# A hybrid decoder layer: turning states and cached keys in 32x32 blocks on VectorE instead of with TensorE transposes

## The chip, the cores and the metric

The kernel runs on one core of one Trainium2 chip. The metric is the time of one execution in device microseconds; several executions are run and the median is given. A profile of one execution gives the span from its first to its last instruction, which is a little shorter than the execution's time.

## The reference

One inference step of one decoder layer, all in float32, for two groups of tokens at once: a prompt of 512 tokens and 8 samples of 4 tokens each, so 544 columns of 1024 features.

```python
proj = rmsnorm(x) @ w_in                      # x_r | q | k | v | two gates
xc, conv_state = causal_dwconv(x_r, lru_conv_prev, conv_w, conv_b)     # width 4
lru_out, h_last = rg_lru(xc, lru_h0, ...)     # 8 block-diagonal gate groups, a scan over time
attn = band_attention(q, [k_cache, k], [v_cache, v], ...)   # window 128, sinks, relative bias
m = (sigmoid(g_A) * (lru_out @ w_lru_o) + sigmoid(g_B) * (attn @ w_attn_o)) @ w_out
x = x + rmsnorm(m)
u, ffn_state = causal_dwconv(rmsnorm(x) @ w_up, ffn_prev, ffn_conv_w, ffn_conv_b)   # width 3
x = x + rmsnorm((gelu(u_gate) * u_val) @ w_down)
```

Beside the new x, the step returns its states, with the time or sample index as rows and the features contiguous: the last LRU state and the last three pre-convolution rows (`s_lru_h`, `s_lru_conv`, 8 and 24 rows of 1024 for the samples; `p_lru_h`, `p_lru_conv`, 1 and 3 rows for the prompt), the key and value windows, and the last two rows of the feed-forward convolution (`s_ffn_conv`, 16 rows of 8192 for the samples; `p_ffn_conv`, 2 rows). The same states of the step before are inputs, in the same layout (`state_lru_h`, `state_lru_conv`, `cache_win_k`, `state_ffn_conv`).

## The kernel before

Inside the kernel, features lie on the 128 partitions and tokens along the free dimension. The states come and go with features contiguous, so each must be turned. Before the change TensorE does this, multiplying by an identity matrix (`pe.transpose`), and VectorE or ScalarE copies the result out of PSUM:

- `params` (L599): 8 transposes of the LRU states (`ps_st`, L604), copied by VectorE into `stT` (L610).
- `sample_attn` (L867), once for each half `g` of the samples: 8 transposes of cached keys (`pkc`, L881), copied by ScalarE into `kcT` (L886), which the score products `pss` read.
- `lru_states` (L1025): two times 4 transposes of the new LRU states (`plr`, L1030), copied by VectorE into the raw buffer `lru_rows` (L1032), which four transfers issued by GpSimd (L1033 to L1036) write out.
- `ffn_prev` (L1508): 8 transposes of the old convolution rows (`psf`, L1513), copied by ScalarE into `sfT` (L1514).
- `ffn_states` (L1734): two times 8 transposes, of the new convolution rows of the samples (`pfs`, L1741) and of the prompt (`pfp`, L1742), copied by ScalarE (L1744, L1746) and written out by transfers that GpSimd issues (L1747, L1748).

Every large product is done in three float32r products (high by high, high by low, low by high): weights are loaded by SyncE into one of five raw buffers (`RAW`, 4 KB a partition), ScalarE writes the rounded high part (L283, L1462), VectorE the rest (L290, and `sub`, L168).

**Order of work.** The order on TensorE is written out by hand throughout, that of ScalarE, VectorE and GpSimd in the mixer too (until `mixer.close()`, L1147), and that of ScalarE and VectorE again in the feed-forward part. SyncE everywhere, GpSimd after the mixer, and ScalarE and VectorE between the two parts are put in order by the scheduler, which goes by the order of emission and its own estimates. The main loop emits one product step after another (`step`, L344; `slot`, L1589). After each, `tick` lets side generators run whose time has come: `start_at(t, gen)` starts one, and `yield k` puts its next piece k steps later. A step in the mixer is 24 matmuls; in the feed-forward part a slot of 12 matmuls counts half a step. Projections empty one of three PSUM buffers (`psm`, used by `PM`), other products and transposes use five (`psx`, `PX`). Slots of the pool `S` (53) hold most activations.

Feed-forward tiles come in pairs `p_` = 0 to 31, a value tile j = `p_` and a gate tile j = 32 + `p_`. `states(j)` (L1543) takes the old rows of tile j out of `sfT`, with m = j // 8 and c = j % 8, and puts the new rows in the same place. From `p_` = 6 on, a pair takes seven half-size products ("a11" to "a22") whose weight sums VectorE and accumulating transfers on GpSimd's queue form (`sums`, L1443; transfers L1450 and L1451). The last pair's convolution, gating and split follow the last products closely; then come eight last column tiles (`down`, with weights `dl`) and the final norms.

Of the kernel before, what the change touches and what calls it, by code (L numbers as in the profile page):

```python
# [11 lines left out]
F32 = mybir.dt.float32  # L12
# [111 lines left out]
def hawk_step(ctx, tc, I, O):  # L124
# [466 lines left out]

    st_rows = [S(f"st_rows{z}") for z in range(2)]
    for z, t_ in enumerate(st_rows):
        zs = slice(512 * z, 512 * z + 512)
        nc.sync.dma_start(out=t_[0:24, 0:512], in_=I["state_lru_conv"][0, :, :, zs].rearrange("b i d -> (b i) d"))
        nc.sync.dma_start(out=t_[24:32, 0:512], in_=I["state_lru_h"][0, :, zs])
    stT = cp.tile([P, KD, 32], F32, name="stT")

    def params():  # L599
        ps = PX("ps_rows")  # L600
        pe.transpose(ps[:, 0:96], rows_a[:, :], ident[:96, :96])
        px = PX("ps_st")
        for k in range(KD):
            pe.transpose(px[:, k * 32:(k + 1) * 32], st_rows[k // 4][:32, (k % 4) * P:(k % 4 + 1) * P], ident[:32, :32])  # L604
        for z in range(2):
# [3 lines left out]
        dve.tensor_copy(fv, ps[:, 128:384])  # L609
        dve.tensor_copy(stT, px[:, 0:256].rearrange("p (k r) -> p k r", k=KD))  # L610
        yield 2
# [255 lines left out]
    def sample_attn(g):  # L867
        raws, kcT = [], []
        for nme in ("cache_win_k", "cache_win_v"):
            t_ = RAW(f"{nme}{g}").rearrange("p (b x) -> p b x", b=4)  # L870
            nc.sync.dma_start(out=t_, in_=I[nme][0, 4 * g:4 * g + 4].rearrange("b j k d -> j b (k d)"))
            raws.append(t_)
        kraw, vraw = raws
        yield 2
        pxs = []
        for half in range(2):
            px = PX(f"pkc{g}{half}")
            for b in range(2):
                for kv in range(NKV):
                    c0 = (2 * b + kv) * P  # L880
                    pe.transpose(px[:, c0:c0 + P], kraw[:, 2 * half + b, kv * HD:(kv + 1) * HD], ident)  # L881
            pxs.append(px)
# [50 lines left out]

    stage = cp.tile([P, KD, 36], F32, name="stage")
    L = Full("l", HALF2)
# [68 lines left out]
    def lru_scan(c):  # L1004
# [17 lines left out]
        pool.tensor_copy(stage[:, c, 27:28], hs[:, SEQ - 1:SEQ])  # L1022
        pool.tensor_copy(stage[:, c, 28:36], hv[:, :, 3])

    def lru_states():  # L1025
        o_t = rp.tile([36, D], F32, tag="raw", name="lru_rows")
        for hf in range(2):
            px = PX(f"plr{hf}")
            for j in range(4):
                pe.transpose(px[:36, j * P:(j + 1) * P], stage[:, 4 * hf + j, :], ident)  # L1030
            yield
            dve.tensor_copy(o_t[:, hf * 512:(hf + 1) * 512], px[:36, :])  # L1032
        pool.dma_start(out=O["p_lru_conv"][0, 0], in_=o_t[0:3, :])  # L1033
        pool.dma_start(out=O["s_lru_conv"][0].rearrange("b i d -> (b i) d"), in_=o_t[3:27, :])
        pool.dma_start(out=O["p_lru_h"][0], in_=o_t[27:28, :])
        pool.dma_start(out=O["s_lru_h"][0], in_=o_t[28:36, :])  # L1036
        yield

# [314 lines left out]


    QL = 32 // CH - 1
    XOF = {"a11": "b11", "a12": "b21", "p2": "t2", "p3": "t3", "p1": "t1", "p4": "b22", "a22": "t4"}
# [145 lines left out]

    sfT = fp.tile([P, KD, 16, 8], F32, name="sfT")
    stage_p = fp.tile([P, KD, 2, 8], F32, name="stage_p")
# [3 lines left out]
    def ffn_prev():  # L1508
        for kk in range(2):
            px = PX(f"psf{kk}")  # L1510
            for j in range(4):
                k = 4 * kk + j
                pe.transpose(px[:, j * P:(j + 1) * P], sf_rows[:, k * P:(k + 1) * P], ident)  # L1513
            act.copy(sfT[:, 4 * kk:4 * kk + 4].rearrange("p c r m -> p c (r m)"),  # L1514
                     px.rearrange("p (c x) -> p c x", c=4))

# [26 lines left out]
    def states(j):  # L1543

        m, c = j // 8, j % 8
        uv = samples(ut[j])
        sv = sfT[:, c, :, m].rearrange("p (b i) -> p b i", b=DB)
# [185 lines left out]

    def ffn_states():  # L1734
        os_ = O["s_ffn_conv"].rearrange("o b i (m n) -> (o b i m) n", n=D)
        op = O["p_ffn_conv"].rearrange("o b i (m n) -> (o b i m) n", n=D)
        for kk in range(2):
            px = PX(f"pfs{kk}")
            py = PX(f"pfp{kk}")
            for j in range(4):  # L1740
                pe.transpose(px[:, j * P:(j + 1) * P], sfT[:, 4 * kk + j].rearrange("p r m -> p (r m)"), ident)  # L1741
                pe.transpose(py[:16, j * P:(j + 1) * P], stage_p[:, 4 * kk + j].rearrange("p r m -> p (r m)"), ident)  # L1742
            o1, o2 = S(f"ffn_rows_s{kk}"), S(f"ffn_rows_p{kk}")
            act.copy(o1[:, 0:512], px)  # L1744
            yield 0.5
            act.copy(o2[:16, 0:512], py[:16, :])  # L1746
            pool.dma_start(out=os_[:, kk * 512:(kk + 1) * 512], in_=o1[:, 0:512])  # L1747
            pool.dma_start(out=op[:, kk * 512:(kk + 1) * 512], in_=o2[:16, 0:512])  # L1748
            yield

# [3 lines left out]
    for z in range(0, len(early), 2):  # L1754
        for u in range(2):
            for j in early[z:z + 2]:
                plain("e", j, u, 0)
                slot(1, 0, nearly, True)
        if z == 6:
            ffn_prev()  # L1760
    at[0], s_ = nearly - AHEAD, 0
# [5 lines left out]
    for i, x in enumerate(plan):  # L1767
# [11 lines left out]
        if i == len(plan) - 8:  # L1779
            start_at(now[0] + 1, x1_again())  # L1780
            start_at(now[0] + 3, ffn_states())

# [197 lines left out]
```

## Time and profile before

| what | value |
|---|---|
| median of 3 runs | 991.0 us (990.68, 991.0, 991.62) |
| span of the profiled execution | 989.3 us |
| runs above the span of the profiled one | 1.4 to 2.3 us (its own time is not given apart) |
| moved by transfers | 135.62 MB, mean 137 GB/s |
| clock granted to TensorE | 0.998 of full speed |

In the views, `PE` is TensorE, `DVE` VectorE, `ACT` ScalarE, `POOL` GpSimd and `SP` SyncE. A row of the chain gives a start, a duration, an engine and a tile. A row of the timeline adds the operation, its shapes and, in brackets, the idle time of the engine just before and what ended it. A row of the groups gives busy time, mean nanoseconds of one, then idle time before. A row of the waits gives total, count and longest. `L168` is line 168, often that of a helper, so tiles tell more than lines.

### The profile page before, as it was taken

What the parts mean: (1) busy time and instruction counts of PE and PEld (TensorE: products, weight loads), DVE (VectorE), ACT (ScalarE), POOL (GpSimd) and SP (SyncE); (2) the same over time, 40 slices, a digit from 0 to 9 for tenths busy, and PEclk for the clock granted to TensorE, in tenths of its full rate; (3) what the DMA queues carried; (4) which work ended last, traced back from release to release, by engine and by line L of the source; (5) the groups of instructions that cost most, each with busy time, mean ns of one, the idle gap of its engine ahead of it and who ended that gap; (6) DMA issues with size and microseconds to landing.
All of it is one profiled execution on the core that took longest, in us unless ns stands there. A gap on an engine that the chain in (4) does not pass through costs nothing.

```text
span 989.3 us, 20126 instructions
## 1 busy us (share of the span) xinstructions
PE 979.6 (99%) x7780; PEld 971.6 (98%) x7780; DVE 746.8 (75%) x1610; ACT 558.3 (56%) x1356; POOL 160.9 (16%) x271
## 2 busy tenths in 40 slices
PE   9999999999999999999999999999999999999997
PEld 8999999999999999999999999999999999999996
DVE  6777678766848555689786778787888888879866
ACT  6545334468476435556766665555655555556652
POOL 2143000002506341210011010101010101011004
PEclk9999999999999999999999999999999999999999
DMA  7675222323223535236058586867676767668612
GB/s 213 187 231 174 81 70 86 107 86 106 87 66 107 176 113 151 60 129 192 13 126 178 136 180 140 177 143 175 145 169 152 168 152 166 155 154 198 197 47 91
DMA packets 211111, 135.62 MB, mean 137 GB/s; under 512 B 8965, under 2 KB 197133, under 8 KB 210984
## 3 DMA queue, kind: packets, MB, share of 16 engines
q1 hardware_dynamic: 198984, 112.59, 40.0%
q0 software_dynamic: 11920, 19.59, 11.9%
q10 hardware_dynamic: 112, 2.17, 0.6%
q8 instruction: 61, 1.00, 0.4%
q14 instruction: 34, 0.28, 0.1%
HBM read 111.78 MB, written 11.37 MB: 124 GB/s over the span
## 4 chain that ended last, share of the span: by engine, by line
PE 96%; DVE 2%; ACT 1%; issue 0%; DVEq 0%; POOL 0%; ACTq 0%; POOLq 0%
PE pmin L165 22%; PE pmdn L165 17%; PE pux L1525 16%; PE puy L1525 8%; PE pq L1525 6%; PE pmout L165 5%; PE pmao L165 5%; PE pmlo L165 5%; PE puz L1525 4%; PE pg L165 1%; PE psc L165 1%; PE pvp L165 1%; PE ptok L165 1%; PE pt L819 1%; PE ps_warm L165 0%
## 5 line engine op out<-in xcount | busy, mean ns | idle before, releaser
L165 PE MATMUL pmin<-hH,wh_in 128*128 128x256 f32 (+1 forms) x568 | 164.6, 292 | 0.0
L165 PE MATMUL pmin<-hL,wh_in 128*128 128x256 f32 (+1 forms) x568 | 162.3, 288 | 0.0
L165 PE MATMUL pmin<-hH,wl_in 128*128 128x256 f32 (+1 forms) x568 | 159.0, 288 | 0.0
L165 PE MATMUL pmdn<-fH,wh_dn 128*128 128x256 f32 (+1 forms) x448 | 129.2, 288 | 0.0
L165 PE MATMUL pmdn<-fH,wl_dn 128*128 128x256 f32 (+1 forms) x448 | 129.2, 288 | 0.0
L165 PE MATMUL pmdn<-fL,wh_dn 128*128 128x256 f32 (+1 forms) x448 | 128.7, 287 | 0.0
L177 DVE SCALAR_TENSOR_TENSOR uc<-u,fv,uc 128x560 f32<-128x560 f32 x128 | 102.0, 797 | 11.6 <-ACT uc L1556 11.4
L165 PEld LDWEIGHTS pmin<-hH,wh_in 128*128 128x128 f32 x568 | 107.2, 189 | 1.4 <-issue 1.2
L165 PEld LDWEIGHTS pmin<-hL,wh_in 128*128 128x128 f32 x568 | 107.3, 189 | 0.1
L165 PEld LDWEIGHTS pmin<-hH,wl_in 128*128 128x128 f32 x568 | 104.7, 188 | 0.2 <-issue 0.2
L165 PEld LDWEIGHTS pmdn<-fL,wh_dn 128*128 128x128 f32 x448 | 84.4, 188 | 0.0
L165 PEld LDWEIGHTS pmdn<-fH,wl_dn 128*128 128x128 f32 x448 | 84.3, 188 | 0.0
L165 PEld LDWEIGHTS pmdn<-fH,wh_dn 128*128 128x128 f32 x448 | 84.3, 188 | 0.0
L1653 ACT COPY u<-pux 128x272 f32<-128x272 f32 x52 | 20.1, 386 | 84.3 <-PE pux L1525 84.2
L168 DVE TENSOR_TENSOR u<-puy,u 128x240 f32<-128x240 f32 (+2 forms) x78 | 24.7, 344 | 50.0 <-PE puy L1525 33.1
L283 ACT ACTIVATE wh_in<-raw_in 128x512 fp32r<-128x512 f32 x70 | 42.8, 628 | 30.9 <-issue 17.8
L174 DVE TENSOR_TENSOR ft<-ft,pmdn 128x256 f32<-128x256 f32 (+1 forms) x104 | 45.2, 436 | 17.1 <-PE pmdn L165 16.9
L290 DVE TENSOR_TENSOR wl_in<-raw_in,wh_in 128x512 fp32r<-128x512 f32 x70 | 48.0, 697 | 1.0 <-ACT wh_in L283 1.0
L1556 ACT ACTIVATE uc<-u,fv 128x560 f32<-128x560 f32 x64 | 48.3, 756 | 0.0
L1451 POOL DMA_DIRECT2D raw_up_s<-raw_up_s x26 | 22.7, 872 | 101.1 <-DMA raw_up_s<-raw_up__7493 4.6
L168 DVE TENSOR_TENSOR wl_dn<-raw_dn,wh_dn 128x512 fp32r<-128x512 f32 x56 | 38.3, 684 | 0.8 <-ACT wh_dn L1462 0.8
L776 ACT ACTIVATE s<-s,st 128x256 f32<-128x256 f32 (+1 forms) x32 | 15.2, 475 | 39.7 <-DVE st L773 26.9
(777 smaller groups left out, 3400.9 us busy)
## 6 DMA issues: line engine op xcount, KB each, us to landing
raw_in<-in_w_in_dram SPq DMA_DIRECT2D x35, 512.0 KB
raw_dn<-in_w_down_dram SPq DMA_DIRECT2D x56, 256.0 KB
raw_up_s<-in_w_up_dram SPq DMA_DIRECT2D x25, 512.0 KB
raw_up_s<-raw_up_s POOLq DMA_DIRECT2D x26, 256.0 KB, 5.5
raw_ao<-in_w_attn_o_dram SPq DMA_DIRECT2D x8, 512.0 KB
raw_lo<-in_w_lru_o_dram SPq DMA_DIRECT2D x8, 512.0 KB
raw_out<-in_w_out_dram SPq DMA_DIRECT2D x8, 512.0 KB
xdram<-xn POOLq DMA_DIRECT2D x8, 272.0 KB, 9.7
```

Source lines behind the costliest of these rows:

```text
L165: pe.matmul(out, l, r, start=start, stop=stop)
L168: dve.tensor_tensor(out=out, in0=a, in1=b, op=ALU.subtract)
L174: dve.tensor_tensor(out=out, in0=a, in1=b, op=ALU.add)
L177: dve.scalar_tensor_tensor(out=out, in0=a, scalar=s_, in1=b, op0=op0, op1=op1)
L283: act.activation(hl[0], raw, AF.Copy)
L290: (eng or dve).tensor_tensor(out=hl[1], in0=raw, in1=f32(hl[0]), op=ALU.subtract)
L776: act.activation(s3[:, j, :], s3[:, j, :], AF.Exp, bias=ng[:, j:j + 1], accum_out=sm[:, j:j + 1])
L819: pe.transpose(pt[:, (2 * ch + j) * P:(2 * ch + j + 1) * P], s3[:, j, ch * P:(ch + 1) * P], ident)
L1451: pool.dma_start(out=w["p4"], in_=w["p2"], accum_op=ALU.add)
L1525: pe.matmul(ps[:, :HN], w, x, start=start and k == 0 and i == 0, stop=stop and k == 3 and i == 2, skip_group_check=True)
L1556: act.activation(yt[j][:, 0:FLATU], u[:, 0:FLATU], AF.Copy, scale=fv[:, j:j + 1])
L1653: act.copy(e[nm_], z)
```

## The change

VectorE can turn 32x32 blocks, each in its place, in one instruction. Transposing a [128, n] tile in this way leaves the order of the blocks wrong, so the transfers put the blocks (32 values, 128 bytes) where they belong. Each of the five places gets a VectorE transpose out of SBUF, and transfers of 128-byte runs, four or eight in place of one.

```diff
-    st_rows = [S(f"st_rows{z}") for z in range(2)]
...
+    strow = drp.tile([32, D], F32, name="strow")
+    nc.sync.dma_start(out=strow[0:24, :], in_=I["state_lru_conv"][0].rearrange("b i d -> (b i) d"))
+    nc.sync.dma_start(out=strow[24:32, :], in_=I["state_lru_h"][0])
+    st_b = S("st_b")
+    def state_blocks():
+        src = strow.rearrange("r (k a c) -> a r k c", a=4, c=32)
+        for a in range(4):
+            nc.sync.dma_start(out=st_b[32 * a:32 * a + 32, 0:256].rearrange("p (k c) -> p k c", k=KD), in_=src[a])
+        yield 4
+        dve.transpose(stT.rearrange("p k r -> p (k r)"), st_b[:, 0:256])
+        yield
...
+    start_at(14, state_blocks())
```

The state rows go from DRAM to DRAM first, so that one tensor holds all 32, and are then loaded by four transfers at step 14 and turned at step 18 (before: step 9).

```diff
     def sample_attn(g):
+        kb = RAW(f"cache_win_k{g}")
+        src = I["cache_win_k"][0, 4 * g:4 * g + 4].rearrange("b (e j) k (a d) -> a k j (b e) d", e=4, a=4)
+        for kv in range(NKV):
+            for a in range(4):
+                nc.sync.dma_start(out=kb[32 * a:32 * a + 32, 512 * kv:512 * kv + 512].rearrange("p (x d) -> p x d", d=32),
+                                  in_=src[a, kv])
+        vraw = RAW(f"cache_win_v{g}").rearrange("p (b x) -> p b x", b=4)
...
         yield 2
-                    pe.transpose(px[:, c0:c0 + P], kraw[:, 2 * half + b, kv * HD:(kv + 1) * HD], ident)
-        yield
...
-            act.activation(kt[:, 0:512], pxs[half], AF.Copy)
+            dve.transpose(kt[:, 0:512].rearrange("p (b k x) -> p b k x", b=2, k=NKV), kb4[:, :, 2 * half:2 * half + 2, :])
...
         dve.tensor_copy(pt[:64, 2 * P:3 * P], px[:64, 2 * P:3 * P])
+        yield
         po = PX(f"pso{g}")
```

One step (the copies') is gone ahead of the scores, and a new one stands between the copies of the turned probabilities and the products `pso`, which stay at their step.

```diff
+    stage = cp.tile([P, KD, 64], F32, name="stage")
+    pool.memset(stage, 0.0)
...
     def lru_states():
+        o_t = rp.tile([P, KD, 2, 32], F32, tag="raw", name="lru_rows")
         for hf in range(2):
...
+            dve.transpose(o_t[:, 4 * hf:4 * hf + 4].rearrange("p c g d -> p (c g d)"),
+                          stage[:, 4 * hf:4 * hf + 4].rearrange("p c r -> p (c r)"))
             yield
-        pool.dma_start(out=O["p_lru_conv"][0, 0], in_=o_t[0:3, :])
...
+        for dst, r0, g, n in (("p_lru_conv", 0, 0, 3), ("s_lru_conv", 3, 0, 24), ("p_lru_h", 27, 0, 1), ("s_lru_h", 0, 1, 8)):
...
+            for a in range(4):
+                nc.sync.dma_start(out=d_[a], in_=o_t[32 * a + r0:32 * a + r0 + n, :, g, :])
+            yield
```

The recurrent outputs leave by sixteen transfers that SyncE issues, four in each of four steps, in place of four of GpSimd.

```diff
+    sfT = fp.tile([P, 4, KD, 16, 2], F32, name="sfT")
+    def ffn_prev():
...
+        rows = [S(f"sf_rows{kk}")[:, 0:512] for kk in range(2)]
+        for kk in range(2):
+            for a in range(4):
+                nc.sync.dma_start(out=rows[kk][32 * a:32 * a + 32].rearrange("p (x d) -> p x d", d=32),
+                                  in_=src[a][:, 16 * kk:16 * kk + 16])
+        yield 3
+        for kk in range(2):
+            dve.transpose(sf_groups(2 * kk, 2 * kk + 2), rows[kk])
+            yield 2
...
+    start_at(now[0] + 1, ffn_prev())
     for a in range(2):
         acc = T(f"acc{a}")
...
-    sf_rows = RAW("sf_rows")
-    nc.sync.dma_start(out=sf_rows, in_=I["state_ffn_conv"].rearrange("o b i (m n) -> (o b i m) n", n=D))
...
+        sv = sfT[:, m % 4, c, :, m // 4].rearrange("p (b i) -> p b i", b=DB)
```

The old convolution rows are loaded and turned during the products with `w_out`, out of two `S` slots, no longer out of a raw buffer during the first feed-forward products. `sfT` is laid out by group m % 4, that is `p_` // 8: group g is final once the pairs 8g to 8g + 7 are done.

```diff
+    def ffn_states(g0, g1):
...
+        dve.transpose(o1[:, 0:n], sf_groups(g0, g1))
+        yield 0.5
+        for a in range(4):
+            pool.dma_start(out=os_[a][:, 8 * g0:8 * g1], in_=o1[32 * a:32 * a + 32, 0:n].rearrange("p (x d) -> p x d", d=32))
+        yield 0.5
+        if g1 < 4:
+            return
...
+        dve.transpose(o2[:, 0:P], stage_p.rearrange("p c r m -> p (c r m)"))
+        yield 0.5
+        for a in range(4):
+            for s_ in range(2):
...
+                pool.dma_start(out=op[a][s_], in_=o2[z:z + 16, 0:P].rearrange("p (j d) -> p j d", j=4))
             yield 0.5
...
         if i == len(plan) - 8:
             start_at(now[0] + 1, x1_again())
+            start_at(now[0] + 3, ffn_states(3, 4))
+        for g0, g1, p_ in ((0, 2, 19), (2, 3, 27)):
+            if x == ("s", p_, "a22"):
+                start_at(now[0] + 3, ffn_states(g0, g1))
```

Groups 0 and 1 leave after pair 19, group 2 after pair 27, group 3 and the prompt's rows where all of them left before.

More of the change, by code (lines that the diff above doesn't have):

```diff
@@ L867, in sample_attn @@
     def sample_attn(g):
[L868 to L873, printed above, removed]
-        yield 2
[L875 to L882, printed above, removed]
-        yield
+        kcT = []
+        kb = RAW(f"cache_win_k{g}")
[5 more added lines that the diff above has]
+        vraw = RAW(f"cache_win_v{g}").rearrange("p (b x) -> p b x", b=4)
+        nc.sync.dma_start(out=vraw, in_=I["cache_win_v"][0, 4 * g:4 * g + 4].rearrange("b j k d -> j b (k d)"))
+        yield 2
+        kb4 = kb.rearrange("p (k b x) -> p k b x", k=NKV, b=4)
         for half in range(2):
             kt = S(f"kcT{g}{half}")
-            act.activation(kt[:, 0:512], pxs[half], AF.Copy)
+            dve.transpose(kt[:, 0:512].rearrange("p (b k x) -> p k b x", b=2, k=NKV), kb4[:, :, 2 * half:2 * half + 2, :])
             kcT.append(kt)
@@ L1022, in lru_scan @@
         pool.tensor_copy(stage[:, c, 27:28], hs[:, SEQ - 1:SEQ])
[L1023 removed]
+        pool.tensor_copy(stage[:, c, 32:40], hv[:, :, 3])
     def lru_states():
[L1026 removed]
+        o_t = rp.tile([P, KD, 2, 32], F32, tag="raw", name="lru_rows")
         for hf in range(2):
[L1028 to L1030 removed]
+            dve.transpose(o_t[:, 4 * hf:4 * hf + 4].rearrange("p c g d -> p (c g d)"),
+                          stage[:, 4 * hf:4 * hf + 4].rearrange("p c r -> p (c r)"))
             yield
[L1032 to L1037 removed]
+        for dst, r0, g, n in (("p_lru_conv", 0, 0, 3), ("s_lru_conv", 3, 0, 24), ("p_lru_h", 27, 0, 1), ("s_lru_h", 0, 1, 8)):
+            d_ = O[dst][0] if dst.endswith("h") else O[dst][0].rearrange("b i d -> (b i) d")
+            d_ = d_.rearrange("r (c a d) -> a r c d", a=4, d=32)
+            for a in range(4):
+                nc.sync.dma_start(out=d_[a], in_=o_t[32 * a + r0:32 * a + r0 + n, :, g, :])
+            yield
     def once(f, *args):
@@ L1732, in x1_again @@
                 yield 0.5
-    def ffn_states():
+    def ffn_states(g0, g1):
         os_ = O["s_ffn_conv"].rearrange("o b i (m n) -> (o b i m) n", n=D)
-        op = O["p_ffn_conv"].rearrange("o b i (m n) -> (o b i m) n", n=D)
[L1737 to L1744, printed above, removed]
+        os_ = os_.rearrange("(r g) (c a d) -> a r (g c) d", g=4, a=4, d=32)
+        n = 256 * (g1 - g0)
+        o1 = S(f"ffn_rows_s{g0}")
+        dve.transpose(o1[:, 0:n], sf_groups(g0, g1))
[5 more added lines that the diff above has]
+            return
+        op = O["p_ffn_conv"].rearrange("o b i (m n) -> (o b i m) n", n=D)
+        op = op.rearrange("r (j s a d) -> a s r j d", s=2, a=4, d=32)
+        o2 = S("ffn_rows_p")
+        dve.transpose(o2[:, 0:P], stage_p.rearrange("p c r m -> p (c r m)"))
+        yield 0.5
+        for a in range(4):
+            for s_ in range(2):
+                z = 32 * a + 16 * s_
+                pool.dma_start(out=op[a][s_], in_=o2[z:z + 16, 0:P].rearrange("p (j d) -> p j d", j=4))
             yield 0.5
[L1746 to L1749, printed above, removed]
     consumed(0, 0)
```

28 lines of the change are left out of this document (5 added, 23 removed).

## The prediction

> **What bounds the kernel now.** I read the page first (busy shares, then the shares of the chain that ended last), then the waits of TensorE, then the chain in order of time around every transpose that the change takes away.
>
> ```profile
> PE 979.6 (99%) x7780; PEld 971.6 (98%) x7780; DVE 746.8 (75%) x1610; ACT 558.3 (56%) x1356; POOL 160.9 (16%) x271
> ...
> PE 96%; DVE 2%; ACT 1%; issue 0%; DVEq 0%; POOL 0%; ACTq 0%; POOLq 0%
> ```
>
> ```profile
> PE pm_first L165 <- DVE wh_in L285: 1.1, 1, 1.1
> PE ps_warm L165 <- POOL ones L219: 1.0, 1, 1.0
> PE pmdn L165 <- DVE ft L174: 0.6, 1, 0.6
> PE pst_f L165 <- DVE accx L174: 0.3, 1, 0.3
> ```
>
> A busy share of 99% would not prove a bound by itself, since matmuls overlap; the other two views do. The chain is TensorE for 96% of the span, and TensorE waits four times, 3.0 us in all. So TensorE time that is taken out anywhere shortens the run one for one, except just ahead of one of these waits, where the removed work was only cover. Two waits lie at the start; the third, 0.6 us on VectorE's ft, has to be looked at, because a removed group stands right ahead of it.
>
> **What the change removes.** Fifty-six transposes on TensorE. The chain prices each group with the slow restart of the matmul behind it.
>
> ```profile
> 41.71 0.61 PE ps_st L604 x8
> ...
> 159.25 0.87 PE pkc L881 x8
> ...
> 179.59 0.87 PE pkc L881 x8
> ```
>
> ```profile
> 352.38 0.44 PE plr L1030 x4
> ...
> 355.81 0.44 PE plr L1030 x4
> ```
>
> ```profile
> 455.28 0.87 PE psf L1513 x8
> ```
>
> ```profile
> 949.36 0.11 PE pfs L1741
> ...
> 950.12 0.11 PE pfp L1742
> ```
>
> States 0.61, cached keys 2 x 0.87 = 1.74, recurrent states 2 x 0.44 = 0.88, old conv states 0.87, second half of the new conv states 8 x 0.11 = 0.87 (first and last of eight rows stand above). Together 4.97 us, all on the chain. The first half of the new conv states is the exception.
>
> ```profile
> 941.80 0.27 PE L1741 MATMUL pfs<-ident,sfT 128*128 128x128 f32 x1
> ...
> 942.59 0.38 PE L165 MATMUL pmdn<-fH,wh_dn 128*128 128x288 f32 x1
> ```
>
> ```profile
> 929.79 0.40 ACT u L1653
> ...
> 940.97 0.93 DVE z L177 x2
> ...
> 944.53 0.37 DVE ft L174
> 945.04 1.84 PE pmdn L165 x12
> ```
>
> It fills 0.79 us at 941.80. But from 929.79 to 945.04 the chain runs over ScalarE and VectorE (the last column tiles being convolved, gated and split), and TensorE's work there only hides it, 0.6 us too little. Without these eight transposes TensorE comes 0.8 to 0.9 us earlier to the same ft and waits that much longer: 1.4 to 1.5 us in place of 0.6, gain nothing. The ft that ends the wait empties the PSUM buffer (of three) that the next product needs. The new VectorE transpose of group 3 is emitted one slot behind that ft and the two splits that follow it, so it does not lengthen the chain; were it one slot ahead, the loss would be its own time, at most 0.4.
>
> **What it adds on VectorE.** Transposes of 512, 512, 512, 512 elements per partition (keys), 256 (states), 512 and 512 (old conv states), 256 and 256 (recurrent), 512, 256, 256 and 128 (new conv states). The trace shows no such operation. Nearest rows, the element-wise operation of the same size and the slowest VectorE operation per element:
>
> ```profile
> L168 DVE TENSOR_TENSOR wl_s_p<-raw_up_s,wh_s_p 128x512 fp32r<-128x512 f32 x52 | 35.6, 685 | 0.0
> ...
> L1013 DVE TENSOR_TENSOR_SCAN hs<-rg,xc 128x568 f32<-128x568 f32 x8 | 13.6, 1695 | 1.6 <-POOL xc L1010 1.6
> ```
>
> That is 0.69 us for 512 elements, or, at the scan's 3.0 ns per element, 1.5. I take 0.69, since a transpose has no element that waits for the one before it. The copies that go (of VectorE in the states and recurrent states, of ScalarE elsewhere) I count at nothing. The keys are the tightest place: 2 x 0.69 = 1.4 us in a step that lasts 3.19 us on TensorE.
>
> ```profile
> 158.40 0.69 DVE L290 TENSOR_TENSOR wl_in<-raw_in,wh_in 128x512 fp32r<-128x512 f32 x1
> ...
> 162.99 0.42 DVE L171 TENSOR_TENSOR ga<-pmin,rep 128x256 f32<-128x256 f32 x1 [1.66 <-PE pmin L165]
> ```
>
> ```profile
> 163.31 3.19 PE pmin L165 x24
> ```
>
> VectorE sits idle 1.66 us just behind, waiting for TensorE, so 1.4 is absorbed and 3.0 (the upper end) leaves 1.4 over, which the weights split two tiles ahead cover. The keys, turned ahead of the split at 158.40, are ready by about 160; the scores that read them move one step up, to about 162.4 (163.31 less the 0.87 removed). The old conv states' two transposes fall among gaps like this one, before the first norm chain:
>
> ```profile
> 399.37 0.44 DVE L174 TENSOR_TENSOR acc<-acc,sq_wo 128x272 f32<-128x272 f32 x1 [2.58 <-ACT sq_wo L1182]
> ```
>
> Cost zero; if the scheduler put them into VectorE's chain further on, 2 x 0.69 = 1.4 us.
>
> **What it adds in transfers.** About 19,100 packets of 128 bytes: 8 x 512 for each half of the keys, 4,096 for the old conv states, 4,096 + 512 for the new ones, 1,152 for recurrent outputs, 1,024 for the states.
>
> ```profile
> q1 hardware_dynamic: 198984, 112.59, 40.0%
> q0 software_dynamic: 11920, 19.59, 11.9%
> ```
>
> ```profile
> DMA to landing us min/median/max: 2.3/2.3/2.4
> ```
>
> Queue 1 spends 0.400 x 16 x 989.3 / 198984 = 31.8 ns per packet (566 bytes on average); by bytes alone 128 would take 7.2 ns; queue 0, with larger and accumulating packets, takes 0.119 x 16 x 989.3 / 11920 = 158 ns. I take 31.8, the row of the same queue and kind of load. Then 4,096 packets on 16 engines, 256 on each, take 8.1 us, and about 2.3 more to land (the 256 KB row above).
>
> ```profile
> 137.73 0.37 SPq L871 DMA_DIRECT2D cache_win_k<-in_cache_win_k_dram  x1
> ```
>
> ```profile
> 164.76 0.37 SPq L871 DMA_DIRECT2D cache_win_k<-in_cache_win_k_dram  x1
> ```
>
> ```profile
> 178.02 0.68 DVE L290 TENSOR_TENSOR wl_in<-raw_in,wh_in 128x512 fp32r<-128x512 f32 x1
> ```
>
> First half: eight issues of 0.37 from 137.73, landed by 148.1, wanted by VectorE before 158.40. Second: landed by 175.2, wanted about 178.0 (the transposes stand next to this split). Old conv states: three steps, 9 us, from issue to first use, and their first half needs 4.1 + 2.3. So VectorE never waits, by 10, 3 and 3 us. Behind such a wait would queue the emptying of the projections' PSUM and the low splits of weights; TensorE would notice after the two steps that are split ahead, some 5 us. The Trainium skill (DMA: Bandwidth & Descriptors, Specifications) says that transfers under 512 B are read-modify-written and lose line rate. As a doubling, which is my estimate from that page, the second half of the keys would land near 183.3, 5 us late, at the edge of that cover, and the sum would lose at most about 1 us.
>
> SyncE also gets the sixteen small issues of the recurrent states, which GpSimd issued before, spread over four steps; behind them wait loads of w_out, and the raw buffer they hold comes free some three steps later.
>
> ```profile
> 363.89 0.99 SPq L259 DMA_DIRECT2D raw_out<-in_w_out_dram  x2
> ```
>
> ```profile
> 380.67 0.62 ACT L283 ACTIVATE wh_out<-raw_out 128x512 fp32r<-128x512 f32 x1
> ```
>
> The loads of 363.89, held until about 373, land near 378 and are first read at 380.67: cost zero, margin 2 to 3 us. GpSimd's memset of the larger stage and the states' detour over DRAM come long before any reader.
>
> **The sum.** 989.3 - 4.97 = 984.3 us of span. The three runs lie 1.4 to 2.3 us above the span of the profiled one; I apply the difference to their median: 991.0 - 5.0 = **986.0 us**. A measurement of this kernel can tell about 0.2%, 2 us, from no change.
>
> **Rivals.** *The whole 5.8.* If the chain before 945 gets shorter because ScalarE loses its copies, the first half counts too: 991.0 - 5.8 = 985.2. Against it: the copy of the first half starts only at the end of that chain. Chance 0.12.
>
> *GpSimd's queue.* Groups 0 and 1 of the new conv states are issued by GpSimd between the accumulating transfers that make the weight sums.
>
> ```profile
> 701.48 0.87 POOL L1450 DMA_DIRECT2D raw_up_s<-raw_up__9582  x1 [11.01 <-ACT wh_s_a L1462]
> 706.18 0.87 POOL L1451 DMA_DIRECT2D raw_up_s<-raw_up_s  x1 [3.83 <-DMA raw_up_s<-raw_up__9582]
> ```
>
> ```profile
> 708.88 0.61 ACT L1462 ACTIVATE wh_s_p<-raw_up_s 128x512 fp32r<-128x512 f32 x1
> ```
>
> ```profile
> L681 POOL DMA_DIRECT2D rrep<-rscr x4 | 4.4, 1112 | 1.7 <-DMA rscr<-rvec 1.7
> ...
> L1747 POOL DMA_DIRECT2D out_dram<-ffn_rows_s x2 | 1.1, 572 | 24.0 <-ACT ffn_rows_s L1744 24.0
> ```
>
> The first sum lands about 706.1 and is read at 708.88: 2.7 us of slack. An issue takes 0.57 us for 128 runs and 1.11 for 256; carried on, 2.2 for 512, and four take 8.8 us. If they stand ahead of the sum's issue, ScalarE reads 6 us late, and what it empties for TensorE with it; four split units cover part. Price about 3 us: 988 to 989. For it: the slot after the pair falls near the sum's issue; against it: GpSimd idles 11 us there. Chance 0.20.
>
> *Late runs of 128 bytes (slower).* If a packet costs 100 ns, 256 of them take 25.6 us. VectorE, which executes in order, waits for the first keys until 165.6 (7 late, 2 after cover), for the second keys 14 (9 after cover), and the old conv states hold the first norm chain some 4: 15 us against 5 gained, 1001. It decides from about 85 ns on. For it: 158 ns in queue 0, and the skill's rule above points this way; against it: 31.8 in the queue that is used. Chance 0.12.
>
> That the transposes on TensorE stay cannot be; that the other buffer lifetimes cost something is in the upper range.
>
> **How the numbers follow.** Forecast 0.56, the full gain 0.12, GpSimd 0.20, late runs 0.12. Faster by over 0.2% are the first two and about a third of GpSimd's: 0.75. Within 0.2%: the rest of that, 0.13. Slower: 0.12. The range reaches from 984.9 (full gain, and the runs' scatter) to 989.5 (GpSimd's price, or 1.4 for misplaced transposes, 0.4 at the end and 1 for the keys); it leaves out the late runs and a little of GpSimd.
>
> **What would show it.** Right: no transposes on TensorE in these five places, the wait on ft at 1.4 to 1.5 us and no other new wait of TensorE, VectorE's transposes near 0.69 us with no idle time ended by a DMA, sums read as before. Wrong: VectorE idle behind the loads of the keys (late runs), idle of ScalarE ended by an accumulating transfer (GpSimd), a TensorE wait on pss, pst_m or pst_f, or a wait on ft that stays 0.6.

## The result, and the profile after

| | median of runs | span of the profiled execution |
|---|---|---|
| before | 991.03 us (4 runs, 990.68 to 991.62) | 989.3 us |
| after | 985.55 us (4 runs, 985.52 to 985.62) | 983.7 us |

The ratio is 0.9944, with an interval of 0.9930 to 0.9958: 5.5 us faster, where 5.0 were forecast. Three lines of the page after, in the order of its parts (busy time, queue 1 of the transfers, shares of the chain that ended last):

```profile
PE 973.2 (99%) x7724; PEld 965.4 (98%) x7724; DVE 751.3 (76%) x1620; ACT 551.0 (56%) x1346; POOL 166.2 (17%) x284
...
q1 hardware_dynamic: 212780, 112.87, 40.9%
...
PE 92%; DVE 4%; ACT 2%; issue 1%; DVEq 0%; POOL 0%; ACTq 0%; POOLq 0%
```

TensorE has lost its 56 instructions and 6.4 us of busy time, VectorE has gained 4.5 us, ScalarE has lost 7.3. The chain holds less TensorE than before, 92%, since more of it now runs over VectorE and ScalarE. The waits of TensorE show where:

```profile
PE pmdn L165 <- DVE ft L174: 1.2, 2, 0.8
PE pm_first L165 <- DVE wh_in L285: 1.1, 1, 1.1
PE ps_warm L165 <- POOL ones L219: 1.0, 1, 1.0
PE pq L1532 <- DVE wl_q L168: 0.5, 1, 0.5
PE pst_f L165 <- DVE accx L174: 0.3, 1, 0.3
```

The wait on ft has doubled, as forecast, and there is one that was not forecast, on `wl_q`. Since TensorE executes the same matmuls in the same order in nearly the whole kernel, the start of one matmul in both timelines tells how far ahead the kernel after is at that place. I worked out this table from such pairs:

| the matmul behind | starts before | starts after | ahead by | gained here | forecast |
|---|---|---|---|---|---|
| the start | 38.40 | 38.33 | 0.07 | | |
| states | 57.06 | 56.24 | 0.82 | 0.75 | 0.61 |
| both halves of the keys | 200.11 | 197.63 | 2.48 | 1.66 | 1.74 |
| recurrent outputs | 360.87 | 357.46 | 3.41 | 0.93 | 0.88 |
| old conv states | 502.79 | 498.49 | 4.30 | 0.89 | 0.87 |
| the new wait on `wl_q` | 505.99 | 502.12 | 3.87 | -0.43 | 0 |
| the pairs of up-projection tiles | 918.12 | 913.49 | 4.63 | 0.76 | 0 |
| first half of the new conv states | 945.04 | 940.42 | 4.62 | -0.01 | 0 |
| second half | 949.99 | 944.49 | 5.50 | 0.88 | 0.87 |

So the sum came out nearly right, but in part by luck: two terms, 0.43 lost and 0.76 gained, were not in it and offset each other in part. The rows of TensorE's timeline after, at the three waits that count here (start, duration, tile, and in brackets the idle time before and what ended it):

```profile
502.12 0.39 PE L1532 MATMUL pq<-b21H,wl_q 128*128 128x272 f32 x1 [0.45 <-DVE wl_q L168]
...
937.76 0.37 PE L165 MATMUL pmdn<-fH,wh_dn 128*128 128x288 f32 x1 [0.35 <-DVE ft L174]
...
940.42 0.37 PE L165 MATMUL pmdn<-fH,wh_dl 128*128 128x288 f32 x1 [0.83 <-DVE ft L174]
```

The wait on ft is in two pieces, 0.35 where the first half's transposes stood, and 0.83 behind the next product.

The new operations and transfers after, by tile: count, then shortest, median and longest in ns, then the first and the last start.

```profile
L603 DVE STREAM_TRANSPOSE stT<-st_b x1: 446/446/446, 77.7 to 77.7; 128x256 f32<-128x256 f32 x1
```

```profile
L876 SPq DMA_DIRECT2D cache_win_k<-in_cache_win_k_dram x16: 328/487/1413, 136.9 to 168.3; - x16
L884 DVE STREAM_TRANSPOSE kcT<-cache_win_k x4: 660/682/711, 157.9 to 177.1; 128x512 f32<-128x512 f32 x4
```

```profile
L1367 SPq DMA_DIRECT2D sf_rows<-in_state_ffn_conv_dram x8: 486/812/1297, 376.0 to 382.2; - x8
L1371 DVE STREAM_TRANSPOSE sfT<-sf_rows x2: 706/708/711, 382.9 to 391.5; 128x512 f32<-128x512 f32 x2
```

A VectorE transpose costs what an element-wise operation of its size does, 0.66 to 0.71 us for 512 and 0.44 for 256. A transfer of 512 runs of 128 bytes takes SyncE 0.49 us (keys) and 0.81 us (old conv states) to issue, at the median, in place of 0.37.

VectorE's waits on transfers: two of the five places are in this list, and both idle times cost TensorE nothing.

```profile
DVE stT L603 <- DMA st_b<-strow: 2.9, 1, 2.9
...
DVE sfT L1371 <- DMA sf_rows<-in_state_ffn_conv_dram: 0.3, 1, 0.3
```

GpSimd's rows around the first group of the new conv states (L1469 and L1470 issue the accumulating transfers of the weight sums):

```profile
747.08 0.86 POOL L1469 DMA_DIRECT2D raw_up_s<-raw_up__10267  x1 [10.49 <-ACT wh_s_a L1481]
748.26 1.39 POOL L1749 DMA_DIRECT2D out_dram<-ffn_rows_s  x2 [0.32 <-DVE z L177]
751.46 0.93 POOL L1470 DMA_DIRECT2D raw_up_s<-raw_up_s  x1 [1.81 <-DMA raw_up_s<-raw_up__10267]
752.06 1.69 POOL L1749 DMA_DIRECT2D out_dram<-ffn_rows_s  x2
```

Two of the four issues fit in before the first sum has landed, the other two follow the second sum's issue, and GpSimd still idles 1.81 us between. Nothing is late.

### The profile page after: what moved, and what is told of

It reads as the page before. It is cut to its first block, busy times and chain, and to the rows that moved or that the text cites. A ratio compares the mean times of both kernels' runs of the same rounds, so it can differ in the third digit from the quotient of the medians.

```text
span 983.7 us, 20075 instructions
## 1 busy us (share of the span) xinstructions
PE 973.2 (99%) x7724; PEld 965.4 (98%) x7724; DVE 751.3 (76%) x1620; ACT 551.0 (56%) x1346; POOL 166.2 (17%) x284
## 4 chain that ended last, share of the span: by engine, by line
PE 92%; DVE 4%; ACT 2%; issue 1%; DVEq 0%; POOL 0%; ACTq 0%; POOLq 0%
PE pmin L165 22%; PE pmdn L165 17%; PE pux L1532 16%; PE puy L1532 8%; PE pmout L165 5%; PE pmlo L165 5%; PE pmao L165 5%; PE puz L1532 4%; PE pq L1532 2%; DVE uc L177 2%; PE pg L165 1%; PE psc L165 1%; PE pvp L165 1%; PE ptok L165 1%; ACT uc L1563 1%
## 5 line engine op out<-in xcount | busy, mean ns | idle before, releaser
L1470 POOL DMA_DIRECT2D raw_up_s<-raw_up_s x26 | 22.4, 862 | 96.9 <-DMA raw_up_s<-raw_up__8875 4.5
```

The source lines that it names most:

```text
L1470: pool.dma_start(out=w["p4"], in_=w["p2"], accum_op=ALU.add)
```

## The experiments

The open questions were three: whether the first half was cover (and the old conv states too, which the prediction had counted in full), where the 0.8 us between 523 and 918 us came from, and how far the small transfers are from hurting. In the first 90 us a run waits for the first loads by up to 1.0 us more or less, in every kernel. So beside the medians I give the lag against the kernel after: how much later the same matmul starts at 146 us, where that scatter is over, and at 975 us. The difference of the two is what an edit behind 146 us cost.

| kernel | median, us (runs) | against after (985.55) | lag at 146 | lag at 975 | cost |
|---|---|---|---|---|---|
| cover8 | 985.94 (5) | +0.39 | 0.18 | 0.22 | 0.04 |
| path8 | 986.63 (5) | +1.08 | 0.64 | 1.57 | 0.93 |
| conv8 | 986.21 (5) | +0.66 | 0.36 | 0.63 | 0.27 |
| keys_late | 994.31 (5) | +8.76 | -0.02 | 9.16 | 9.18 |
| conv_end | 986.79 (5) | +1.24 | -0.35 | 0.41 | 0.76 |
| x1_early | 985.42 (5) | -0.13 | 0.59 | 0.37 | -0.22 |
| x1_best | 984.63 (5) | -0.92 | 0.99 | 0.15 | -0.84 |
| old_layout | 985.42 (1) | -0.13 | -0.12 | -0.03 | 0.09 |

In the kernels whose edit lies behind 523 us, and in `old_layout`, the lag grows by 0.04 to 0.09 us between 146 and 523 us already, so the costs are good to about 0.1 us.

The kernel before had medians of 990.92 to 991.24 beside these runs.

### Eight transposes put back, in three places

```diff
+    def eight(nm):
+        px = PX(f"px8s{nm}")
+        py = PX(f"px8p{nm}")
+        for j in range(4):
+            pe.transpose(px[:, j * P:(j + 1) * P], sfT[:, j, 0:4].rearrange("p c r m -> p (c r m)"), ident)
+            pe.transpose(py[:16, j * P:(j + 1) * P], stage_p[:, j].rearrange("p r m -> p (r m)"), ident)
```

`cover8` calls it where the first half stood, just ahead of group 3's VectorE transpose; `path8` three half steps later, where the second half stood; `conv8` puts eight transposes of `sfT` where those of the old conv states stood.

> The kernel after, with eight TensorE transposes of the new conv states (their results are not used) put back where the first half of the old output stood, ahead of the down product of 937.76 us. Cover theory: they fill the waits on ft, which fall from 0.35 and 0.83 us to about 0.6 together; the chain of ScalarE and VectorE from 925.19 to 940.42 keeps its 15.2 us; the time stays within 0.3 us of the kernel after, 985.6 to 985.9. Rival (the first half was on the path, and its removal is part of the 5.5 us gained): 0.88 us more, 986.4.

> The kernel after, with the same eight TensorE transposes put in where the second half of the old output stood, some 5 us behind the last wait on ft. By my theory there is no wait behind them that they could fill, so all 0.87 us are added: 986.4. Rival (TensorE has cover there too, since VectorE and ScalarE feed the sums of squares): less than 0.4 us, 985.6 to 985.9.

> The kernel after, with eight TensorE transposes put in where those of the old conv states stood (their results are not used), near 452 us. Theory from the two traces: the gain of 0.88 us there was followed by a new wait of 0.45 us on wl_q near 502, so the transposes were half cover: the wait on wl_q goes, and the time rises by only 0.43 us, to 986.0. Rival, as the prediction had it: all 0.87 are on the path, 986.4, and the wait on wl_q has another cause and stays.

The waits of TensorE on ft and `wl_q` in `cover8`, and its row at the last wait:

```profile
PE pmdn L165 <- DVE ft L174: 0.5, 1, 0.5
PE pq L1532 <- DVE wl_q L168: 0.5, 1, 0.5
```

```profile
940.65 0.37 PE L165 MATMUL pmdn<-fH,wh_dl 128*128 128x288 f32 x1 [0.52 <-DVE ft L174]
```

The eight transposes swallow 0.66 us of the waits and cost 0.04, all of it ahead of 523 us. In `path8` the same eight cost 0.93: the same instructions, some 7 us later. In `conv8` TensorE is 0.86 us later behind the eight (lag 0.38 ahead of them, 1.24 at 455 us), then the wait on `wl_q` is missing from its list and the lag falls to 0.66 at 506 us:

```profile
PE pmdn L165 <- DVE ft L174: 1.2, 2, 0.8
PE ps_warm L165 <- POOL ones L219: 1.0, 1, 1.0
PE pm_first L165 <- DVE wh_in L285: 0.8, 1, 0.8
PE pst_f L165 <- DVE accx L174: 0.3, 1, 0.3
PE pmin L165 <- DVE ks L171: 0.2, 1, 0.2
```

So the cover theory holds in all three places, and the rival of `conv8`, which was the prediction, falls: half or more of the old conv states' transposes was cover for VectorE, 50 us ahead of the place where the wait shows. Between before and after, 0.43 of the 0.89 us was lost again; here 0.58 of 0.86 is swallowed, so that the eight cost 0.28 behind `wl_q` and 0.27 at 975 us, less than the forecast 0.43. The wait that goes was longer than the 0.45 that the profile counts: after, TensorE starts that product 0.74 us behind the one before it, where the products ahead of it follow at 0.12 to 0.13.

### The conv states alone, and the other parts alone

The change is cut in two: `conv_only` has its hunks from `ffn_prev` on, `rest_only` those ahead of it.

> The kernel before with the old and new conv states alone changed (VectorE turns them, the new layout, the groups); recurrent states and cached keys stay on TensorE. By the cover theory it gains 0.43 for the old conv states (0.88 less a new wait on wl_q of about 0.45), nothing for the first half of the new ones, 0.88 for the second: 1.3 us. The pace of TensorE between 523 and 918 us tells where the other 0.8 came from: if from the conv states' layout, the stretch is shorter by 0.8 here too and the time is 991.0 - 2.1 = 988.9; if from the places of the buffers as the other three parts shift them, it is as before and the time is 989.7.

> The kernel before with the recurrent states and the cached keys alone changed; the conv states stay on TensorE. From the landmarks of the two traces: states 0.75, keys 1.6, recurrent outputs 0.9, together 3.2 us: 991.0 - 3.2 = 987.8, and TensorE's pace between 523 and 918 us as before (the 0.8 us belong to the conv states). Rival (the new small transfers or VectorE cost something that the traces do not show): above 988.3. Rival (the pace comes from the shifted buffers of any part): 987.0.

`conv_only` took 989.12 us (11 runs) and `rest_only` 988.17 (7 runs): 1.9 and 2.9 faster than the 991.03 above, 4.8 together, as against 5.5 for the whole (the kernel before had 991.2 beside them, which makes it 5.1). The intervals of the ratios are 0.9971 to 0.9989 and 0.9958 to 0.9980. In `conv_only` the wait on `wl_q` is there, the first half gains nothing and the second 0.88; `rest_only` has neither that wait nor a change in the wait on ft. From 38 us to the end it gains 3.17 us by its matmuls' starts (0.26 behind the kernel before, then 2.91 ahead), as the landmarks had it. Both times lie a little above their forecasts, 988.9 (with the pace) and 987.8. The waits of `conv_only`, then of `rest_only` (whose two others stand in the first 40 us):

```profile
PE pmdn L165 <- DVE ft L174: 1.2, 2, 0.8
...
PE pq L1532 <- DVE wl_q L168: 0.5, 1, 0.5
```

```profile
PE ps_warm L165 <- POOL ones L219: 1.0, 1, 1.0
PE pmdn L165 <- DVE ft L174: 0.6, 1, 0.6
PE pst_f L165 <- DVE accx L174: 0.3, 1, 0.3
...
```

### Where TensorE's pace comes from

Between 523 and 918 us no wait of TensorE changes, and yet the kernel after runs through the same matmuls in less time. Four kernels were made for this; two of them need a diff:

```diff
-    sfT = fp.tile([P, 4, KD, 16, 2], F32, name="sfT")
+    sfT = fp.tile([P, KD, 16, 8], F32, name="sfT")
...
-        return sfT[:, g0:g1].rearrange("p g c r m -> p (g c r m)")
+        return sfT.rearrange("p c r (m g) -> p g (c r) m", g=4)[:, g0:g1]
```

```diff
+    def two_slots():
+        for z in range(2):
+            dve.memset(S(f"two{z}")[:, 0:2], 0.0)
+        yield
+    start_at(now[0] + 1, two_slots())
```

The first is `old_layout`, on the kernel after; the second is `two_slots`, on the kernel before; `before_again` is the kernel before unchanged, and `conv_only` is the one above.

> The kernel before, unchanged, profiled once more. Between 523 and 918 us TensorE never waits in either trace, yet it gains 0.80 us there after the change, though the change takes no instruction out of that stretch. Theory A (the pace of that stretch differs from one execution to the next, whatever the kernel): in this trace the stretch from the pux of 523.51 to the pux of 918.12, 394.61 us before and 393.81 us after, comes out anywhere from 393.8 to 394.6. Rival B (the new layout of the conv states makes TensorE's pace faster): it is 394.6 again. Span by A 988.4 to 989.3 us, by B 989.3.

> The kernel after with the conv states kept in the order of before (column, sample, step, block) in place of groups first; VectorE's transposes write and read them in strides, all else as after. The stretch between 523 and 918 us of before, which took 0.80 us less after and kept that in every kernel with the new conv states, tells its cause. Layout theory (ScalarE's small copies into and out of the states are 14 to 20 ns shorter with the new order, and TensorE's pace follows): the stretch is 0.7 to 0.8 us longer than after and the span near 984.5. Rival (the buffers' places, which this kernel leaves as they are): as after, 983.7 and the run's scatter. VectorE's transposes with strides may take longer than 0.70 us; nothing waits for them.

> The kernel before, and at the step where the kernel after begins to load the old conv states two more tiles are taken from the rotating pool that also holds the operands of the up-projection (each gets a memset of two columns, nothing reads them); all work and its order stay. Between 523 and 918 us TensorE ran 0.80 us shorter after, 0.7 with the conv states alone, as before with the other parts alone, and the layout is not the cause. Theory (the operands' places in SBUF set a few ns of many matmuls): the stretch changes by 0.3 us or more, to about 393.9 if the two slots are all of it, and the time with it to about 990.3. Rival (something else of the conv part, ScalarE's missing copies or the writes in groups): 394.6 and 991.0, as before.

Time for the same 3,140 or so matmuls of that stretch, from their starts in both traces:

| kernel | against | difference, ns |
|---|---|---|
| before_again | before | -1 |
| two_slots | before | -335 |
| conv_only | before | -713 |
| rest_only | before | +114 |
| after | before | -780 |
| old_layout, cover8, path8, x1_early | after | 0, 0, -1, 0 |
| conv_end | after | +27 |
| conv8 | after | +80 |

`before_again` took 991.0 us, with a span of 989.2. The pace repeats to a nanosecond from one execution to another, so theory A of `before_again` falls: it belongs to the kernel. The layout is not it either. `old_layout` keeps the pace, although its copies are as long as before, and its VectorE transposes, which read and write in strides, are longer, 1.12 us for 512 against 0.71:

```profile
L1555 ACT COPY u<-sfT x64: 201/232/240, 455.1 to 933.4; 128x16 f32<-128x16 f32 x64
...
L1371 DVE STREAM_TRANSPOSE sfT<-sf_rows x2: 1099/1116/1133, 383.0 to 391.4; 128x512 f32<-128x512 f32 x2
```

`two_slots` adds two tiny memsets and no other work, and the stretch gets 335 ns shorter. That shows that taking two slots of the rotating pool, so that the later tiles get others, is enough to move TensorE's pace, at 0.1 ns a matmul on average. No hidden wait makes the difference: between before and after, no step from one matmul's start to the next in this stretch changes by more than 11 ns, up or down. It is not shown that this is all of the 780: taking the two slots explains less than half of it. Two other runs bear on the rest: `conv8` takes again the two PSUM buffers that the change gave up (+80), and `conv_end` takes the groups' output slots out of the stretch (+27). The raw buffer that is no longer taken was not tried alone, and why a buffer's place should matter is open. By its time, 990.66 against 990.92 us (ratio 0.9989 to 1.0007), `two_slots` can't be told from before; by its trace it can.

### The keys' slack steps taken away

```diff
+        vraw = RAW(f"cache_win_v{g}").rearrange("p (b x) -> p b x", b=4)
...
+        yield 2
         kb = RAW(f"cache_win_k{g}")
...
                 nc.sync.dma_start(out=kb[32 * a:32 * a + 32, 512 * kv:512 * kv + 512].rearrange("p (x d) -> p x d", d=32),
                                   in_=src[a, kv])
-        vraw = RAW(f"cache_win_v{g}").rearrange("p (b x) -> p b x", b=4)
...
-        yield 2
```

> The kernel after, with each half of the cached keys loaded in the step of its VectorE transposes, two steps later; the values keep their load. In the kernel after the loads last 4.99 and 4.04 us from first issue to last and about 2 more to land, and are wanted 15 and 6 us after that. Theory (the slack steps are what keeps the loads off the path): VectorE now waits for DMA, up to 7 us at each half, behind it the splits of weights, and TensorE, with two steps split ahead, some 5 us, loses 0 to 2 us at each half: 985.6 to 989.6, with a wait of TensorE near 160 or 178 us if it is over 985.9. Rival (SyncE issues far enough ahead anyhow, so that the step does not matter): VectorE idles less than 1 us behind the keys and the time is 985.6.

994.31 us, far above the forecast 985.6 to 989.6, and slower than before (ratio 1.0021 to 1.0046). The rows of the second half: VectorE's transposes, TensorE's first product behind them, and the busy times from 182 to 205 us (length of each stretch, then PE, PEld, DVE, ACT and POOL with counts, the granted clock, transfers).

```profile
187.94 1.30 DVE L884 STREAM_TRANSPOSE kcT<-cache_win_k 128x512 f32<-128x512 f32 x2 [11.41 <-DMA cache_win_k<-in_cache_win_k_dram]
```

```profile
188.71 1.66 PE L165 MATMUL pss<-kcT,qs 128*32 128x256 f32 x8 [6.20 <-DVE kcT L884]
```

```profile
182.00:184.00 2.00, 0.51 (x10) 0.30 (x2) 0.00 (x0) 0.00 (x0) 0.00 (x0) 1.00 0.34 54
184.00:186.00 2.00, 0.00 (x0) 0.00 (x0) 0.00 (x0) 0.00 (x0) 0.00 (x0) 0.56 0.74 118
186.00:190.00 4.00, 1.29 (x8) 0.38 (x8) 2.06 (x4) 0.00 (x0) 0.00 (x0) 0.50 0.29 46
190.00:194.00 4.00, 4.00 (x19) 3.70 (x18) 3.90 (x10) 0.71 (x3) 0.00 (x0) 0.50 0.48 135
194.00:195.00 1.00, 1.00 (x9) 1.00 (x9) 1.00 (x3) 1.00 (x4) 0.00 (x0) 0.76 0.00 0
195.00:205.00 10.00, 10.00 (x83) 10.00 (x82) 8.28 (x29) 4.83 (x18) 0.58 (x4) 1.00 0.36 107
```

The second half was issued from 182.20 us, 17 us later than after: by the profile, SyncE waited 8.5 us ahead of it for the first half's products `pso`, which read the cached values out of a raw buffer. VectorE idled 11.41 us, and TensorE waited 6.20: the cover was 5.2 us, about the 5 of the prediction. Then came a cost that no forecast of mine had: the granted clock fell to 0.50 within 2 us of the start of the wait and stayed there until 194.5 us. TensorE went on at 188.71, so it ran 5.8 us at half speed, which took another 2.9 us of the 9.18. The Trainium skill (TensorE: Matmul & The Clock Gate, Part 1) says that an idle window of some 3.4 us halves the clock, and that it takes a busy window to get it back. This trace agrees on the half and on the busy time, with 5.8 us, though the clock fell sooner than 3.4 us into the wait. At the first half VectorE idled 0.66 us and nothing was lost. The rival falls: loading the keys two steps later, with the later buffer that this brings, costs 9 us.

### All the groups at the end, and a use for the waits that are left

`conv_end` starts all three calls of `ffn_states` at the place of the last one. `x1_early` has one number changed, and `x1_best` one more:

```diff
     def x1_again():
...
-        yield 3
+        yield 2
...
-            start_at(now[0] + 3, ffn_states(3, 4))
+            start_at(now[0] + 5, ffn_states(3, 4))
```

> The kernel after, with all the new conv states turned and written at the end, none in groups before. VectorE gets 0.70 + 0.44 us more near 941 us, where it makes the low splits of the last down weights and adds up ft, and GpSimd eight more issues of 0.6 to 1.0 us. Theory (VectorE is what feeds TensorE in that place): a new wait of TensorE on wl_dl or on pmdn's buffers of 0.3 to 1.1 us: 985.9 to 986.7. Rival (after the wait on ft has ended VectorE has slack, and the grouping is worth nothing): within 0.2 us of the kernel after, 985.4 to 985.8.

> The kernel after, with the TensorE transposes of the first-half output (x1, four groups of four, which stand behind the last wait on ft) one step earlier: two groups of about 0.45 us now stand ahead of the last down products, where TensorE waits 0.35 and 0.83 us for ft. Cover theory: both groups fill those waits, ScalarE's copies of them come behind the last fH in its order, and the time falls by 0.8 to 0.9: 984.7. Rival (the chain of 15.2 us gets longer with the copies, or the loads of x1 come late): 985.5 or more, with a longer chain.

> As x1_early, and the last group of the new conv states turned and written two steps later. In x1_early TensorE gained 0.86 us at the last down products and lost most of it again: ScalarE's last copy of x1 waited 2.21 us for a write of the new conv states to land, because it takes their buffer, and the sums of squares came late behind it. Theory: with the write later that wait goes, and the time falls to 984.7 to 984.9. Rival (the sums of squares themselves are the next bound): 985.3 or more, with a wait of TensorE on the last sum of 0.3 us or more.

In `conv_end` TensorE waits 0.47 us more, in a third piece, on ft: the forecast mechanism. But its median is higher than the forecast 985.9 to 986.7 by a little. The profiled run is the fastest of the five (985.89 to 987.25), so what lengthened the others is not shown. ScalarE has a wait that I had not thought of:

```profile
PE pmdn L165 <- DVE ft L174: 1.7, 3, 0.8
```

```profile
948.13 0.59 ACT L1737 COPY xtok<-px 128x512 f32<-128x512 f32 x1 [2.07 <-DMA out_dram<-ffn_rows_s]
```

In `x1_early` the two groups cost nothing in the waits, TensorE was 0.84 us further ahead at 949 us (lag 0.59 to -0.25), and had given 0.62 of it back at 975, so that the time was 985.42 and not the 984.7 forecast. The same kind of wait stands in its rows, and TensorE waits on the last sum of squares:

```profile
948.26 0.59 ACT L1737 COPY xtok<-px 128x512 f32<-128x512 f32 x1 [2.21 <-DMA out_dram<-ffn_rows_s]
```

```profile
PE pst_o L165 <- DVE acc L174: 0.3, 1, 0.3
```

The copy takes the slot that still holds the turned conv states, whose write has not landed; behind it in ScalarE's order wait the squares. In `x1_best`, with the write two steps later, the wait on `pst_o` is gone, that on ft is down to 0.4, and the lag falls by 0.84 and stays there:

```profile
PE pm_first L165 <- DVE wh_in L285: 0.8, 1, 0.8
PE pq L1532 <- DVE wl_q L168: 0.5, 1, 0.5
PE pmdn L165 <- DVE ft L174: 0.4, 1, 0.4
```

984.63 us: the fastest version, 0.9 us below the kernel after and 0.63% below before (ratio 0.9925 to 0.9950). Its five runs reach from 984.43 to 985.61; the slowest of them is the profiled one, which lost 0.99 us in its first 90.

## Why the prediction was right, and where it was not

**The path.** Right in the main: at the five places TensorE's time came back one for one, 5.1 us against 4.97, though 0.43 of it was lost again further on (below). States gave 0.75 for 0.61 and the keys 1.66 for 1.74; the rest is within 0.05.

**The first half as cover.** Right, and shown by `cover8` and `path8`. From ScalarE's copy of the last pair's product, at 929.79 us before and here

```profile
925.19 0.39 ACT L1660 COPY u<-pux 128x272 f32<-128x272 f32 x1 [0.65 <-PE pux L1532]
```

to the down product that waits for ft at 945.04 and 940.42, the chain takes 15.25 us before and 15.23 after. The rival of the whole gain falls with this, though the time, 985.55, lies a little nearer to its 985.2 than to the forecast 986.0. What the kernel gained beyond the 5.1 us came from the pace, 0.76, less the 0.43 lost on `wl_q`, and not from the first half; that the two cancel in part is luck. The wait was forecast at 1.4 to 1.5 and is 1.18.

**The old conv states.** Wrong. The step that failed is the test "except just ahead of one of these waits": I looked for waits that were in the list, and the list had none behind the old conv states before the one on ft. A place without a wait can still have less slack than what is removed ahead of it. VectorE's chain, from the norm through the operands and the first convolutions to the split `wl_q`, gained only about 0.4 us there while TensorE gained 0.89; the wait of 0.45 shows 50 us later. It could have been seen in rows of before, of VectorE and of TensorE:

```profile
505.25 0.68 DVE L168 TENSOR_TENSOR wl_q<-raw_up__6162,wh_q 128x512 fp32r<-128x512 f32 x1
```

```profile
505.67 0.28 PE L1525 MATMUL pq<-b21L,wh_q 128*128 128x272 f32 x1
505.99 0.40 PE L1525 MATMUL pq<-b21H,wl_q 128*128 128x272 f32 x1
```

The product starts 0.06 us behind the end of its split, 505.93, so there is no slack. TensorE even waits there already: the product starts 0.32 us behind the one before it, where those ahead of it follow at 0.12 to 0.13. The list of waits doesn't show these 0.2 us, because a matmul's modelled duration, 0.28, hides most of them.

**The pace.** Not in the sum at all: 0.76 to 0.80 us. Tiles moved to other buffers are at least part of the cause (`two_slots`), the layout is not, the rest is open.

**The added work.** VectorE's durations were right (0.66 to 0.71 for the 0.69 taken). A 128-byte packet took 13.5 ns on average in queue 1, not 31.8, and one of 512 bytes 29.5. The trace records 14,464 packets of 128 bytes and not the 19,100 forecast, since the new conv states, on GpSimd's queue, stand there in 320 larger ones. By bytes alone, a quarter of the 29.5, a packet of 128 would take 7.4 ns; my doubling would make it 14.7, which is close. The Trainium skill (DMA: Bandwidth & Descriptors, Specifications) has it that transfers under 512 B lose line rate. The trace agrees, with 1.8 times the time per byte. The 256 packets on each engine then take 3.5 us, less than SyncE needs to issue a half: its eight issues last 4.99 and 4.04 us, and set the time. The keys landed some 15 and 6 us ahead of use, not 10 and 3. That VectorE would never wait for a transfer was wrong twice, by 2.9 us at the states, whose detour over DRAM I had put "long before any reader", and 0.3 at the old conv states, both without a cost.

**GpSimd.** The rival did not come: an issue of 512 runs took 0.68 to 1.02 us (two overlap a little in the rows above), not 2.2, and ScalarE's one wait on a sum, 1.5 us before, is gone after. Where the prediction carried a price on by the number of runs, the price did not grow with it.

**Late runs.** The rival did not come, by a factor of six in the price of a packet. `keys_late` shows that its mechanism is real, and that it was priced too low: it left out the clock.

## What to carry to other kernels

Work removed from the bound engine counts only as far as the feeding engines have slack up to the next place where they meet, and that slack has to be read at every place, also where no wait stands in the profile: take the end of the last input against the start of the reader, and the step from the matmul before it against the usual step. Where a wait is left, independent work of the bound engine can be moved into it (0.84 us here), if no buffer that it takes is held by a write under way. Small transfers were cheap here because they were issued two steps early; late, they cost their wait and the clock behind it.

## What the runs showed of the hardware that was not expected

- TensorE's pace changed with the buffers that tiles were given: the same matmuls in the same order took 335 ns less over 395 us when two slots were taken, and 780 ns less with the whole change. It repeats to 1 ns from run to run.
- A VectorE transpose of 512 float32 values per partition took 0.71 us contiguous, 1.12 with strides.
- A wait of TensorE of 6.20 us cost 2.9 more, at a granted clock of 0.50 for 5.8 us behind it.
- A transfer of 512 runs of 128 bytes took SyncE 0.49 us to issue for the keys and 0.81 for the old conv states, at the median; the 512 KB load that stood there before, in runs of 1 KB, took 0.37.
